# Second buffers and other banks for the mixers' calls, reversed columns in their inverse, and the last adaLN vector summed by VectorE in the gate and up stage

## The chip, the core and the metric

The kernel runs on one core of a Trainium2 chip. The core has five engines that run side by side and wait for one another by semaphores: TensorE (matrix products, results into PSUM), VectorE (DVE in the rows), ScalarE (ACT), GpSimd (POOL) and SyncE (SP), whose queue issues most transfers. The metric is the device time of one execution in microseconds (us).

## What is computed

One block of a backbone with depth 1 on 256 latent tokens and 256 context tokens, width 2048. Six modulation vectors come from the conditioning vector; the sixth, `m_x[5]`, is the gate of the last residual. `_mix` projects to four groups of heads: GLA, Gated DeltaNet (GDN), a short convolution and RWKV-7. The scans run in both directions, first over the context, then over the latent tokens from the context's states.

```python
def _modulation(cond, w, bias):
    m = jax.nn.silu(cond) @ w + bias
    return [a[:, None, :] for a in jnp.split(m, 6, axis=-1)]
...
        o_c, ctx_states = _mix(_modnorm(h_c, norm1_g[l], m_c[0], m_c[1]), h_c.shape[1], zero, lp)
        o_x, _ = _mix(_modnorm(h_x, norm1_g[l], m_x[0], m_x[1]), GRID_W, ctx_states, lp)
        h_x = h_x + m_x[2] * o_x
        h_x = h_x + m_x[5] * _swiglu(_modnorm(h_x, norm2_g[l], m_x[3], m_x[4]), ffn_w_gu[l], ffn_w_down[l])
...
    return _rmsnorm(h_x, final_g)
```

## The kernel before

**Stages.** A first stage (to about 205 us) makes the first two modulation vectors, the norm of the context and eleven early projection tiles. The mixers (to about 1130) hold 16 RWKV directions (4 pairs of heads, 2 directions, context and latent), 8 GDN calls and 4 GLA calls, with the other projections between them. Then come the output projection, gate and up (about 1280 to 1765), down, and the last norm.

**Weights.** A weight tile arrives as float32 (`wraw`), ScalarE rounds it to a high part (`wh`), VectorE subtracts (`wl`), and TensorE makes three products: high by high, high by low, low by high. A projection (`proj`) makes 48 such products of 256 columns from four tiles, in a bank of the pair "big". In gate and up the tiles are 1024 wide (`wide`: four raw buffers, two of each part), while the small set of the mixers (`narrow`: six raw buffers, three of each part) is used in the first turn alone.

**The feed.** Vectors 3, 4, 2 and 5 are fed in this order into the projections: `ada_pieces` gives 64 pieces and a finish for each; `proj` takes two pieces for each of its four weight tiles. A piece is a load of 256 KB into a `wraw` buffer and four products (float32, so two passes) with 32 rows of output, in the bank "ob". The finish of 2 and 5 writes the row to memory, from where it is spread over the partitions (`gate_bc`).

**The inverse.** RWKV and GDN invert four triangular 128x128 matrices a call (`inverse`): VectorE takes the 16x16 blocks of the diagonal (a masked product and a reduction), TensorE spreads their rows (`pr`), and 15 steps of a product and an addition on VectorE make the blocks' inverses (`w_`, `Xc`). RWKV has one kind of triangle in a call. GDN has two lower and two upper ones, and steps over the two kinds apart. Levels of 32 (and 64) then double the blocks on TensorE (`pv`, `px`, `pxt`).

**Banks.** `PB` gives PSUM banks by tag: stream "a" (RWKV) has two "ea" and one "la"; stream "b" (GDN, GLA) one "eb" and one "lb"; the projections have two "big"; the feed has "ob". Eight in all.

**What sets the order.** The code is recorded in the order of the list `ORDER` (with offsets in priority), and a scheduler then gives each engine one fixed order, by priority and by when a buffer is free. A tile with one buffer is given out again when its last reader is done. An engine works strictly in its order, so an instruction that waits holds all behind it.

## Time and profile before

| | us |
|---|---|
| median of three timed runs | 2026.64 |
| lowest and highest | 2023.53, 2029.68 |
| the profiled execution | 2028.87 |
| its span | 2027.1 |
| TensorE busy in the span | 1915.4 |
| VectorE busy | 1343.7 |
| ScalarE busy | 994.5 |

The span is that of the core's instructions. An engine is busy while one of its instructions runs; overlapping instructions count once. TensorE's instructions overlap and their ends are modelled, so a busy TensorE is not one at its peak. The chain that ended last is followed back from the last instruction, at each step to what released it.

### The profile page before, as it was taken

How to read it: one execution, taken by the hardware profiler on the slowest of the kernel's cores; microseconds unless marked ns; L12 is line 12 of the kernel's file. 1: busy time of each engine (PE TensorE's matmuls, PEld its weight loads, DVE VectorE, ACT ScalarE, POOL GpSimd, SP SyncE). 2: the span in 40 equal slices, each digit the busy share in tenths (PEclk: the TensorE clock that was granted, in tenths of full speed). 3: DMA queues.
4: the chain of work that ended last, by engine and by line, in shares of the span. 5: the costliest groups of instructions: out<-in, count | busy, mean ns of one | idle time of the engine just before them, and what ended most of it. 6: DMA issues, size and time to landing. Idle time of an engine off the chain costs nothing.

```text
span 2027.1 us, 37228 instructions
## 1 busy us (share of the span) xinstructions
PE 1915.4 (94%) x13799; PEld 1633.6 (81%) x13800; DVE 1343.7 (66%) x3488; ACT 994.5 (49%) x2029; POOL 161.5 (8%) x199
## 2 busy tenths in 40 slices
PE   5988999799999999999999999899999999999998
PEld 3776877588877878989989978788888888888886
DVE  3446758788788758989897766655555555545554
ACT  2225535555455345465644555555555555544444
POOL 0001001001001000110110000210101010100000
...
GB/s 340 402 292 218 181 224 253 118 138 140 168 204 188 156 193 205 115 110 108 82 118 120 168 184 210 116 187 186 187 187 187 187 187 186 186 231 197 191 194 156
DMA packets 162391, 375.07 MB, mean 185 GB/s; under 512 B 17937, under 2 KB 44049, under 8 KB 157089
## 3 DMA queue, kind: packets, MB, share of 16 engines
...
q8 instruction: 108, 1.77, 0.4%
...
HBM read 360.68 MB, written 11.94 MB: 184 GB/s over the span
## 4 chain that ended last, share of the span: by engine, by line
PE 69%; DVE 10%; DMA 5%; ACT 3%; issue 2%; POOL 0%; SPq 0%; ACTq 0%; DVEq 0%
PE acc L209 36%; PE big L209 12%; PE la L209 7%; PE lb L209 4%; PE ea L209 4%; DVE wl L197 3%; DMA wraw<-in_w_in 3%; PE eb L209 2%; PE ob L209 2%; ACT wh L192 2%; DMA wraw<-in_ada_later 2%; DVE ivaXc L197 1%; DVE ivaw L197 1%; DVE ivbw L197 0%; DVE ivbXc L197 0%
## 5 line engine op out<-in xcount | busy, mean ns | idle before, releaser
L197 DVE TENSOR_TENSOR wl<-wraw,wh 128x512 fp32r<-128x512 f32 x856 | 569.9, 692 | 425.4 <-ACT wh L192 420.7
L192 ACT ACTIVATE wh<-wraw 128x512 fp32r<-128x512 f32 x856 | 510.1, 625 | 543.6 <-PE acc L209 187.3
L209 PE MATMUL acc<-n,wh 128*128 128x512 f32 x1408 | 493.6, 399 | 2.5 <-ACT wh L192 2.5
L209 PE MATMUL acc<-n,wl 128*128 128x256 f32 x1408 | 383.3, 282 | 0.3 <-DVE wl L197 0.3
L209 PE MATMUL big<-nh,wh 128*128 128x256 f32 x1056 | 320.4, 304 | 1.7 <-ACT xs L192 1.3
L209 PE MATMUL big<-nh,wl 128*128 128x256 f32 x1056 | 309.6, 294 | 1.4 <-DVE wl L197 1.4
L209 PEld LDWEIGHTS acc<-n,wh 128*128 128x128 f32 x1408 | 260.0, 189 | 59.6 <-ACT wh L192 2.8
L209 PE MATMUL big<-nl,wh 128*128 128x256 f32 x1056 | 307.7, 292 | 0.0
L209 PEld LDWEIGHTS acc<-n,wl 128*128 128x128 f32 x1408 | 267.2, 190 | 9.7 <-DVE wl L197 1.3
L209 PEld LDWEIGHTS big<-nh,wh 128*128 128x128 f32 x1056 | 200.4, 190 | 27.2 <-issue 19.4
L209 PEld LDWEIGHTS big<-nh,wl 128*128 128x128 f32 x1056 | 200.3, 190 | 8.0 <-issue 2.9
L209 PEld LDWEIGHTS big<-nl,wh 128*128 128x128 f32 x1056 | 200.2, 190 | 5.2 <-issue 4.1
L209 PE MATMUL acc<-wl,hH 128*128 128x512 f32 x352 | 137.1, 389 | 0.0
L209 PE MATMUL acc<-wh,hH 128*128 128x512 f32 x352 | 137.0, 389 | 0.0
L209 PE MATMUL acc<-wh,hL 128*128 128x512 f32 x352 | 137.0, 389 | 0.0
L209 PE MATMUL ob<-wraw,sc 128*32 128x128 f32 x2048 | 106.4, 281 | 16.0 <-DMA wraw<-in_ada_later 12.4
L209 PEld LDWEIGHTS ob<-wraw,sc 128*32 128x32 f32 x2048 | 51.1, 108 | 52.2 <-DMA wraw<-in_ada_later 18.4
L197 POOL TENSOR_TENSOR hL<-sg,hH 128x256 fp32r<-128x256 f32 x44 | 44.6, 1013 | 454.2 <-ACT hH L192 454.2
L209 PEld LDWEIGHTS acc<-wl,hH 128*128 128x128 f32 x352 | 66.1, 188 | 14.2 <-DVE wl L197 0.4
L209 PEld LDWEIGHTS acc<-wh,hL 128*128 128x128 f32 x352 | 66.1, 188 | 13.8
L209 PEld LDWEIGHTS acc<-wh,hH 128*128 128x128 f32 x352 | 66.1, 188 | 13.7
L197 DVE TENSOR_TENSOR wl<-wr,wh 128x1408 fp32r<-128x1408 f32 x16 | 26.0, 1624 | 42.4 <-ACT wh L192 42.4
(468 smaller groups left out, 3123.9 us busy)
## 6 DMA issues: line engine op xcount, KB each, us to landing
wraw<-in_w_gu SPq DMA_DIRECT2D x174, 512.0 KB, 3.1
...
wraw<-in_ada_later SPq DMA_DIRECT2D x256, 256.0 KB, 3.9
...
```

What stands on the lines that cost most here:

```text
L192: A.activation(o, i, AF.Copy)
L197: (e or V).tensor_tensor(out=o, in0=a, in1=b, op=op)
L209: return TE.matmul(o, l, r, start=start, stop=stop)
```

## The change

- The sixth vector (5 in the feed's numbers) is no longer fed to TensorE in the mixers. In gate and up, 64 pieces of 128x512 of its weights are loaded from the third turn on, two recorded in each turn, into the narrow raw buffers; VectorE multiplies each by the conditioning value of its rows and adds it to one of four accumulators, which take two of the three narrow buffers of each part. After the stage TensorE sums the accumulators over the partitions with four products with `ones`, and VectorE adds the bias.
- The inverse gets its diagonal blocks by four ScalarE copies of 32 partitions (`dq`) and two VectorE operations on 64 columns. The upper triangles are held with their columns reversed, so both kinds go through the same 15 steps, on all four matrices at once; the columns are turned back when the blocks are spread.
- `pr` moves from the bank "l" to "e" of its stream; `pxt` of the inverse and `pe` of GDN move from "e" to "big".
- `rw_kt`, `rw_na`, `gd_tok`, `gd_dl` and the ring `bdLM` get a second buffer. The space comes from `ident`, which is left out of the second copy of the constants, and from one tag for two outputs.

The diff, cut to its core (the other hunks repeat second buffers, or shift offsets of constants by 128):

```diff
@@ -154,9 +156,12 @@
     first = a[:, :, 0:2].transpose(3, 1, 0, 2, 4).reshape(KT * P, KT * 2 * P)
-    later = w[:, 2 * D:].reshape(KT, P, 4, 4, 4, P).transpose(2, 4, 0, 1, 3, 5).reshape(4 * 4 * KT * P, 512)
+    later = w[:, 2 * D:5 * D].reshape(KT, P, 3, 4, 4, P).transpose(2, 4, 0, 1, 3, 5).reshape(3 * 4 * KT * P, 512)
+    last = w[:, 5 * D:].reshape(KT * P, 4, 512).transpose(1, 0, 2).reshape(4 * KT * P, 512)
+    later = np.concatenate([later, last])
     return np.ascontiguousarray(first), np.ascontiguousarray(later)
...
@@ -296,13 +301,13 @@
             row = wraw()
-            if ci in (2, 5):
+            if ci == 2:
                 G.memset(row, 0.0)
                 for g in range(4):
                     nc.sync.dma_start(row[32 * g:32 * g + 1, :], ada_b[0:1, ci * D + g * 512: ci * D + (g + 1) * 512])
                 tt(row, ps, row, ADD)
                 for g in range(4):
-                    nc.sync.dma_start(gate_dram[ci // 4:ci // 4 + 1, g * 512:(g + 1) * 512], row[32 * g:32 * g + 1, :])
+                    nc.sync.dma_start(gate_dram[0:1, g * 512:(g + 1) * 512], row[32 * g:32 * g + 1, :])
                 return
...
@@ -652,11 +659,13 @@
             for u, low in enumerate(lowers):
                 groups.setdefault(low, []).append(u)
 
-            t5 = mk(mx, [P, 4, 8, 16], iv + "L", 1)
-            tt(t5, nL.rearrange("p u (b c) -> p u b c", c=16),
-               blk16.unsqueeze(1).unsqueeze(3).to_broadcast([P, 4, 8, 16]), MUL)
+            dq = mk(mx, [P, 4, 32], iv + "Q", 1)
+            for q in range(4):
+                sl = slice(32 * q, 32 * q + 32)
+                acopy(dq[sl], nL[sl, :, sl])
             dg = mk(mx, [P, 4, 16], iv + "D", 1)
-            V.tensor_reduce(out=dg, in_=t5.rearrange("p u b c -> p u c b"), axis=mybir.AxisListType.X, op=ADD)
+            ts(dg, dq[:, :, 0:16], even, MUL)
+            stt(dg, dq[:, :, 16:32], odd, dg, MUL, ADD)
 
             dx = mk(mx, [P, 4, 15], iv + "d", 1)
             for low, us in groups.items():
...
@@ -667,32 +676,27 @@
             sel = mk(mx, [P, 4, 8, 15], iv + "R", 1)
             tt(sel, bcast(dx, 2, 8), row8.unsqueeze(1).unsqueeze(3).to_broadcast([P, 4, 8, 15]), MUL)
 
-            pr = PB([P, 480], "l")
+            pr = PB([P, 480])
             mm(pr, ones16, sel.rearrange("p u i j -> p (u i j)"))
             bc_ = mk(mx, [P, 4, 8, 15], iv + "C", 1)
             acopy(bc_.rearrange("p u i j -> p (u i j)"), pr)
             Xc = mk(mx, [P, 4, 16], iv + "Xc", 1)
-            G.tensor_copy(Xc, bcast(id16, 1, 4))
+            for low, us in groups.items():
+                G.tensor_copy(Xc[:, us[0]:us[-1] + 1], bcast(id16 if low else id16r, 1, len(us)))
             w_ = mk(mx, [P, 4, 16], iv + "w", 1)
             for st in range(15):
-                step = []
-                for low, us in groups.items():
-
-                    n, u = 15 - st, slice(us[0], us[-1] + 1)
-                    if low:
-                        i = 15 - st
-                        js, e = slice(0, n), bc_[:, u, st, 0:n] if i >= 8 else bc_[:, u, i, 14:14 - n:-1]
-                    else:
-                        i = st
-                        js, e = ((slice(15, i, -1), bc_[:, u, i, 0:n]) if i < 8 else
-                                 (slice(i + 1, 16), bc_[:, u, 15 - i, i:15]))
-                    tt(w_[:, u, js], e, Xc[:, u, i:i + 1].to_broadcast([P, len(us), n]), MUL)
-                    step.append((u, js))
-                for u, js in step:
-                    tt(Xc[:, u, js], Xc[:, u, js], w_[:, u, js], ADD)
+                n = i = 15 - st
+                e = bc_[:, :, st, 0:n] if i >= 8 else bc_[:, :, i, 14:14 - n:-1]
+                tt(w_[:, :, 0:n], e, Xc[:, :, i:i + 1].to_broadcast([P, 4, n]), MUL)
+                tt(Xc[:, :, 0:n], Xc[:, :, 0:n], w_[:, :, 0:n], ADD)
             X = mk(mx, [P, 4, P], iv + "X", 2)
-            tt(X.rearrange("p u (b c) -> p u b c", c=16), bcast(Xc, 2, 8),
-               blk16.unsqueeze(1).unsqueeze(3).to_broadcast([P, 4, 8, 16]), MUL)
+            for low, us in groups.items():
+                us_ = slice(us[0], us[-1] + 1)
+                tt(X[:, us_].rearrange("p u (b c) -> p u b c", c=16),
+                   bcast(Xc[:, us_] if low else Xc[:, us_, ::-1], 2, 8),
+                   blk16.unsqueeze(1).unsqueeze(3).to_broadcast([P, len(us), 8, 16]), MUL)
             nxt = iv + "XT", 1 if len(levels) == 2 and rhs is not None else 2
             XT = mk(mx, [P, 4, P], *nxt)
             pt = PB([P, 4, P], "l")
...
@@ -729,7 +733,7 @@
                 if not last and (rhs is None or b != levels[-2]):
-                    pxt = PB([P, 4, P])
+                    pxt = PB([P, 4, P], "big")
                     for c in range(4):
...
@@ -943,12 +947,12 @@
                     TE.transpose(pk[:, c], f2(KK[:, c]), ident)
-                kt_ = mk(mx, [P, 4, P], "rw_kt", 1)
+                kt_ = mk(mx, [P, 4, P], "rw_kt", 2)
                 acopy(kt_, pk)
 
                 w = P if s == 1 else 64
                 def turned(t, tag):
-                    pt, o = PB([P, 4, P]), mk(mx, [P, 4, P], tag, 1)
+                    pt, o = PB([P, 4, P]), mk(mx, [P, 4, P], tag, 2 if tag == "rw_na" else 1)
                     for c in range(4):
...
@@ -1064,7 +1068,7 @@
                 l2(q, P ** -0.5)
-            tok = mk(mx, [P, 4, P], "gd_tok", 1)
+            tok = mk(mx, [P, 4, P], "gd_tok", 2)
             pt = PB([P, 4, P])
...
@@ -1084,7 +1088,7 @@
                 mm(pbc[:, d], ident[:, 32 + r:33 + r].to_broadcast([P, P]), sm["smd"][d])
-            dl = mk(mx, [P, 4, P], "gd_dl", 1)
+            dl = mk(mx, [P, 4, P], "gd_dl", 2)
             R = mk(mx, [P, 4, 2, P], "gd_R", 1)
...
@@ -1125,7 +1129,7 @@
                     ts(Fg[:, u].rearrange("p a b -> p (a b)")[:, :w], src, sm["nbe"][:, d, h, c:c + 1], MUL)
-                pe = PB([P, 2, 2, P])
+                pe = PB([P, 2, 2, P], "big")
                 for c in range(2):
...
@@ -1338,10 +1342,10 @@
         rings = rws.enter_context(tc.tile_pool(name="rings", bufs=1, reuse_waits="tile"))
-        bdLM = Ring(rings, "bdLM", [P, 4, 2, 2, 64], 1)
+        bdLM = Ring(rings, "bdLM", [P, 4, 2, 2, 64], 2)
         bdKh = Ring(rings, "bdKh", [P, 4, 2, 64], 1)
         bdE = Ring(rings, "bdE", [P, 4, 2, 64], 1)
-        for ci in (3, 4, 2, 5):
+        for ci in (3, 4, 2):
             feed += ada_pieces(ci, lambda shape: mk(pb, shape, "ob", 1), mx)
...
@@ -1460,7 +1464,25 @@
     p3 = ctx.enter_context(tc.tile_pool(name="p3", bufs=1, reuse_waits="tile"))
     hH = mk(p3, [P, FT, T], "hH", 1, F32R)
     hL = mk(p3, [P, FT, T], "hL", 1, F32R)
+    gacc = [mk(narrow[0], [P, 512], t, narrow[2]) for t in ("wh", "wh", "wl", "wl")]
+    def gate_piece(i):
+        kt, q = divmod(i, 4)
+        raw = mk(narrow[0], [P, 512], "wraw", narrow[3])
+        r0 = ((3 * 4 + q) * KT + kt) * P
+        nc.sync.dma_start(raw, ada_later[r0:r0 + P, :])
+        if kt == 0:
+            ts(gacc[q], raw, sc[:, 0, 0:1], MUL)
+        else:
+            stt(gacc[q], raw, sc[:, kt, 0:1], gacc[q], MUL, ADD)
+    gate_todo = list(range(4 * KT))
     for f in range(FT):
+        if f > 1:
+            for i in gate_todo[:2]:
+                gate_piece(i)
+            del gate_todo[:2]
 
         pg = [mk(ps2, [P, 2, T], "acc", 8) for _ in range(2)]
         for k0, nk, bufs in ((0, 8, wide), (8, 4, narrow), (12, 4, narrow)) if f == 0 else ((0, 8, wide), (8, 8, wide)):
...
@@ -1493,7 +1515,12 @@
     with tc.issue_after(silu.ins):
         A.preload_act_table_set("natural_log_exp_and_others")
     g5 = mk(p5, [P, D], "g5")
-    gate_bc(1, g5)
+    nc.sync.dma_start(g5, ada_b[0, 5 * D:6 * D].partition_broadcast(P))
+    for q in range(4):
+        ps = mk(ps2, [P, 512], "acc", 8)
+        mm(ps, ones, gacc[q])
+        sl = slice(q * 512, (q + 1) * 512)
+        tt(g5[:, sl], ps, g5[:, sl], ADD)
     fg = mk(p5, [P, D], "fg")
     nc.sync.dma_start(fg, final_g.partition_broadcast(P))
     ss = [mk(p5, [P, 4], f"ss{j}", 1) for j in range(2)]
```

TensorE, during one GDN inverse over the context (`lb` products with `ivb` tiles) beside an RWKV inverse (`la`, `iva`). Before:

```order
L209 MATMUL lb_5675<-ivbX_5657,ivbW_5673 128x128 x4
L209 MATMUL eb_5681<-ivbW_5673,ivbX_5657 128x128 x4
L209 MATMUL la_5461<-rw_na_5372,ivaX_5457 128x64 x4
L209 MATMUL big_6911<-nl_831_4125,wh_6974 128x256
L209 MATMUL big_6911<-nh_830_4124,wl_6975 128x256
L209 MATMUL lb_5691<-ivbXT_5686,ivbL_5689 128x128 x4
L209 MATMUL la_5468<-ivaW_5466,ivaL_5459 128x64 x4
L209 MATMUL big_6911<-nh_834_4134,wh_6974 128x256
L209 MATMUL big_6911<-nl_835_4135,wh_6974 128x256
L209 MATMUL big_6911<-nh_834_4134,wl_6975 128x256
```

Now, in the same call:

```order
L214 MATMUL lb_5605<-ivbX_5586,ivbW_5603 128x128 x4
L214 MATMUL big_5611<-ivbW_5603,ivbX_5586 128x128 x4
L214 MATMUL la_5929<-ivaXT_5920,ivaL_5927 128x128 x4
L214 MATMUL lb_5621<-ivbXT_5616,ivbL_5619 128x128 x4
L214 MATMUL la_5936<-ivaX_5918,ivaW_5934 128x128 x2
L1228 MATMUL eb_5737<-ident_64,gd_k_5725 128x128 x2
L214 MATMUL la_5936<-ivaX_5918,ivaW_5934 128x128 x2
L214 MATMUL lb_5628<-ivbX_5610,ivbW_5626 128x128 x3
L214 MATMUL eb_5742<-gd_kq_5721,gd_dl_5740 128x256
L214 MATMUL lb_5628<-ivbX_5610,ivbW_5626 128x128
L214 MATMUL big_5634<-ivbW_5626,ivbX_5610 128x128
```

Between the two streams' products stood projection products (`big<-nl,wh` and the like); now the products of a GLA call (`eb`) stand there, `pxt` is in "big", and no projection product.

VectorE, at the start of the first GDN inverse (`ivb`) beside an RWKV inverse. Before, with the reduction and the first step on two matrices twice (`128x2x15 x2`):

```order
L659 TENSOR_REDUCE ivbD_2781<-ivbL_2779 128x64
L197 TENSOR_TENSOR wl_2440<-wraw_2437,wh_2439 128x512
L201 TENSOR_SCALAR ivbd_2783<-ivbD_2781,consts_89 128x30 x2
L206 SCALAR_TENSOR_TENSOR ivbd_2783<-ivbD_2781,consts_89,ivbd_2783 128x30 x2
L197 TENSOR_TENSOR ivbL_2866<-gd_dl_2764,consts_89 128x512
L197 TENSOR_TENSOR wl_2475<-wraw_2472,wh_2474 128x512
L197 TENSOR_TENSOR ivbR_2788<-ivbd_2783,consts_89 128x480
L197 TENSOR_TENSOR ivaR_1633<-ivad_1630,consts_89 128x480
L197 TENSOR_TENSOR ivaL_1681<-bdLM_254_1533,consts_89 128x512
L197 TENSOR_TENSOR wl_2505<-wraw_2502,wh_2504 128x512
L197 TENSOR_TENSOR ivbw_2796<-ivbC_2792,ivbXc_2794 128x2x15 x2
L203 TENSOR_SCALAR rw_z_1754<-ea_1755,par_63 128x256
```

Now, from the second of the two operations that replace the reduction:

```order
L211 SCALAR_TENSOR_TENSOR ivbD_2794<-ivbQ_2789,consts_89,ivbD_2794 128x64
L206 TENSOR_SCALAR ivaD_1633<-ivaQ_1628,consts_89 128x64
L206 TENSOR_SCALAR ivbd_2797<-ivbD_2794,consts_89 128x30 x2
L211 SCALAR_TENSOR_TENSOR ivbd_2797<-ivbD_2794,consts_89,ivbd_2797 128x30 x2
L211 SCALAR_TENSOR_TENSOR ivaD_1633<-ivaQ_1628,consts_89,ivaD_1633 128x64
L202 TENSOR_TENSOR ivbR_2802<-ivbd_2797,consts_89 128x480
L206 TENSOR_SCALAR ivad_1636<-ivaD_1633,consts_89 128x60
L211 SCALAR_TENSOR_TENSOR ivad_1636<-ivaD_1633,consts_89,ivad_1636 128x60
L202 TENSOR_TENSOR wl_2450<-wraw_2447,wh_2449 128x512
L202 TENSOR_TENSOR ivaR_1639<-ivad_1636,consts_89 128x480
L202 TENSOR_TENSOR ivbw_2811<-ivbC_2806,ivbXc_2808 128x4x15
L202 TENSOR_TENSOR ivbXc_2808<-ivbXc_2808,ivbw_2811 128x4x15
```

The reduction is gone, `ivaD` and `ivbD` are made from `ivaQ` and `ivbQ`, and a step is one product and one addition on four matrices (`128x4x15`).

VectorE in gate and up, about one turn of the loop (`wl` are the low parts, two halves each). Before:

```order
L197 TENSOR_TENSOR wl_16259<-wraw_16256,wh_16258 128x512 x2
L197 TENSOR_TENSOR wl_16267<-wraw_16264,wh_16266 128x512 x2
L197 TENSOR_TENSOR wl_16320<-wraw_16317,wh_16319 128x512 x2
L197 TENSOR_TENSOR ga_16304<-acc_16206,ga_16304 128x256
L197 TENSOR_TENSOR wl_16328<-wraw_16325,wh_16327 128x512 x2
L197 TENSOR_TENSOR up_16305<-acc_16207,up_16305 128x256
L197 TENSOR_TENSOR sg_16306<-ga_16304,up_16305 128x256
L197 TENSOR_TENSOR wl_16368<-wraw_16365,wh_16367 128x512 x2
```

Now, where the sixth vector is summed (`wh_15567` and the like are its accumulators):

```order
L202 TENSOR_TENSOR wl_16268<-wraw_16265,wh_16267 128x512 x2
L202 TENSOR_TENSOR ga_16246<-acc_16148,ga_16246 128x256
L211 SCALAR_TENSOR_TENSOR wh_15567<-wraw_17867,sc_82,wh_15567 128x512
L202 TENSOR_TENSOR wl_16276<-wraw_16273,wh_16275 128x512 x2
L202 TENSOR_TENSOR up_16247<-acc_16149,up_16247 128x256
L211 SCALAR_TENSOR_TENSOR wh_15568<-wraw_17870,sc_82,wh_15568 128x512
L202 TENSOR_TENSOR sg_16248<-ga_16246,up_16247 128x256
L211 SCALAR_TENSOR_TENSOR wl_15569<-wraw_17982,sc_82,wl_15569 128x512
L202 TENSOR_TENSOR wl_16316<-wraw_16313,wh_16315 128x512 x2
L211 SCALAR_TENSOR_TENSOR wl_15570<-wraw_17985,sc_82,wl_15570 128x512
L202 TENSOR_TENSOR wl_16324<-wraw_16321,wh_16323 128x512 x2
L211 SCALAR_TENSOR_TENSOR wh_15567<-wraw_18097,sc_82,wh_15567 128x512
```

One or two sums stand ahead of each pair of splits; the 64 are spread over about the first fourteen turns.

## Rows read from the trace of the kernel before

**Rows 1.** page, its first line.

```profile
span 2027.1 us, 37228 instructions
```

**Rows 2.** stretch, length, busy us (instructions) of PE, PEld, DVE, ACT, POOL; clock, DMA.

```profile
205.00:640.00 435.00, 402.65 (x3715) 335.64 (x3714) 332.02 (x1136) 223.01 (x495) 29.27 (x46) 0.96 0.57 176
640.00:800.00 160.00, 153.99 (x1449) 128.18 (x1447) 119.50 (x368) 70.45 (x144) 13.31 (x16) 1.00 0.63 196
800.00:1130.00 330.00, 317.07 (x2418) 294.97 (x2418) 284.91 (x886) 176.95 (x374) 36.96 (x44) 1.00 0.35 110
```

**Rows 3.** page, part 4: the chain that ended last, by engine.

```profile
PE 69%; DVE 10%; DMA 5%; ACT 3%; issue 2%; POOL 0%; SPq 0%; ACTq 0%; DVEq 0%
```

**Rows 4.** tile ob: busy in 640 to 800; the finishing additions, first and last.

```profile
640.00:800.00 160.00, 27.09 (x512) 12.60 (x512) 1.37 (x2) 0.00 (x0) 1.00 0.63 196
L197 DVE TENSOR_TENSOR wraw<-ob,wraw x2: 682/686/691, 640.4 to 795.8; 128x512 f32<-128x512 f32 x2
```

**Rows 5.** the chain by line in 640 to 800, then in 800 to 1000.

```profile
by line: DMA wraw<-in_w_in 15.4%; PE big L209 13.1%; PE la L209 12.8%; PE lb L209 6.6%; PE ob L209 5.5%; DVE wl L197 5.3%; ACT wh L192 4.6%; PE ea L209 4.2%; DMA wraw<-in_ada_later 3.9%; issue 3.8%; DVE ivaXc L197 3.4%; DVE ivaw L197 2.6%; 
by line: PE big L209 25.1%; PE la L209 18.1%; PE lb L209 9.6%; PE ea L209 8.0%; DVE wl L197 7.1%; PE eb L209 6.0%; issue 3.1%; ACT wh L192 1.5%; DMA gd_rk<-xr_d_k 1.5%; DVE ivaw L197 1.3%; DVE ivaXc L197 1.2%; DVE ivaX L197 1.1%; DVE ivbD L
```

**Rows 6.** waits in 640 to 800, ScalarE's, then SyncE's queue: us, times, longest.

```profile
ACT wh L192 <- DMA wraw<-in_w_in: 22.8, 16, 3.3
SPq L292 <- PE ob L209: 25.5, 25, 2.4
```

**Rows 7.** VectorE in 205 to 1130: shape, count, busy us, mean ns, idle before.

```profile
L197 DVE TENSOR_TENSOR wl<-wraw,wh 128x512 fp32r<-128x512 f32 x231 | 160.9, 698 | 59.7 <-ACT wh L192 55.7 <-PE ob L209 1.6 <-PE eb L209 0.8
L197 DVE TENSOR_TENSOR ivaL<-bdLM,consts 128x512 f32<-128x512 f32 x47 | 33.1, 704 | 0.0
L659 DVE TENSOR_REDUCE ivaD<-ivaL 128x64 f32<-128x512 f32 x15 | 15.4, 1024 | 0.1
L201 DVE TENSOR_SCALAR ivad<-ivaD,consts 128x60 f32<-128x60 f32 x16 | 3.9, 246 | 0.1
L206 DVE SCALAR_TENSOR_TENSOR ivad<-ivaD,consts,ivad 128x60 f32<-128x60 f32 x16 | 4.4, 274 | 0.0
L197 DVE TENSOR_TENSOR ivbw<-ivbC,ivbXc 128x30 f32<-128x30 f32 x16 | 2.3, 182 | 0.7 <-ACT ivbC L192 0.7
L197 DVE TENSOR_TENSOR ivbXc<-ivbXc,ivbw 128x2 f32<-128x2 f32 x16 | 2.0, 155 | 0.0
L197 DVE TENSOR_TENSOR ivaw<-ivaC,ivaXc 128x60 f32<-128x60 f32 x16 | 3.7, 228 | 4.6 <-ACT ivaC L192 4.4
L197 DVE TENSOR_TENSOR ivaXc<-ivaXc,ivaw 128x4 f32<-128x4 f32 x16 | 3.1, 192 | 0.1
```

**Rows 8.** ScalarE in 205 to 1130: a small copy, and a wait.

```profile
L192 ACT ACTIVATE gd_S<-lb 128x128 f32<-128x128 f32 x24 | 6.6, 274 | 15.9 <-PE lb L209 15.8
ACT rw_kt L192 <- PE la L209: 5.2, 6, 1.9
```

**Rows 9.** three other stretches, columns as in rows 2; the last is GB/s.

```profile
700.00:750.00 50.00, 49.06 (x449) 40.32 (x448) 23.42 (x56) 19.00 (x38) 1.61 (x3) 1.00 0.45 143
800.00:950.00 150.00, 144.13 (x1092) 132.98 (x1092) 137.12 (x461) 82.65 (x174) 19.73 (x23) 1.00 0.35 108
1400.00:1450.00 50.00, 50.00 (x285) 43.48 (x284) 27.75 (x49) 25.59 (x53) 4.08 (x4) 1.00 0.56 186
```

**Rows 10.** the chain in 815 to 835: start us, us, what.

```profile
821.88 11.26 PE big L209 x94
```

**Rows 11.** VectorE's 128x512 operation; ones products; a gap in gate and up.

```profile
L206 DVE SCALAR_TENSOR_TENSOR gd_qe<-gd_qe,par,gd_tok 128x512 f32<-128x512 f32 x2 | 1.5, 746 | 0.0
L209 PE MATMUL lb<-gd_tok,ones 128*128 128x512 f32 x4 | 2.2, 627 | 0.0
1402.65 1.29 DVE L197 TENSOR_TENSOR wl<-wraw,wh 128x512 fp32r<-128x512 f32 x2 [1.61 <-ACT wh L192]
```

**Rows 12.** page, part 2: GB/s in 40 slices.

```profile
GB/s 340 402 292 218 181 224 253 118 138 140 168 204 188 156 193 205 115 110 108 82 118 120 168 184 210 116 187 186 187 187 187 187 187 186 186 231 197 191 194 156
```

More of the change, by code (lines that the diff above doesn't have):

```diff
@@ L87, in _const_array @@
     add("half", np.concatenate([q < 8, q >= 8], 1))
+    add("side", np.concatenate([i // 16 % 2 == 0, i // 16 % 2 == 1], 1))
+    add("id16r", np.arange(P)[:, None] % 16 == 15 - np.arange(16)[None, :])
     r = np.arange(32)[None, :]
@@ L275, in rsqrt @@
         act(o, o, AF.Exp, scale=-0.5)
-    gate_dram = mk(dram, [2, D], "gated")
+    gate_dram = mk(dram, [1, D], "gated")
     def ada_pieces(ci, bank_of, tmp):
@@ L337, in block_kernel @@
     kp = mix.enter_context(tc.tile_pool(name="kp", bufs=1, reuse_waits="tile"))
-    C = mk(kp, [P, NCONST], "consts")
+    C = mk(kp, [P, NCONST - P], "consts")
     sw = mk(kp, [P, 3072], "sw")
     def cc(name, n=P):
-        return C[:, COFF[name]:COFF[name] + n]
+        return C[:, COFF[name] - P:COFF[name] - P + n]
     lev = {b: cc(f"lev{b}") for b in LEVS}
@@ L351, in block_kernel @@
     lo8, hi8 = cc("half", 2)[:, 0:1], cc("half", 2)[:, 1:2]
+    even, odd = cc("side", 2)[:, 0:1], cc("side", 2)[:, 1:2]
+    id16r = cc("id16r", 16)
     class Ring:
@@ L468, in block_kernel @@
         for i, dst in ((0, C), (1, sw)):
-            nc.sync.dma_start(dst, (consts, small)[i])
+            nc.sync.dma_start(dst, (consts[:, P:], small)[i])
         for f in done:
@@ L1181, in gla @@
             if s == 1:
-                v = mk(mx, [P, 4, 2, 64], "gd_tok", 1)
+                v = mk(mx, [P, 4, 2, 64], "gd_tok", 2)
                 for hh in range(2):
@@ L1197, in gla @@
             else:
-                v = mk(mx, [P, 2, 2, P], "gd_tok", 1)
+                v = mk(mx, [P, 2, 2, P], "gd_tok", 2)
                 for hh in range(2):
@@ L1224, in gla @@
                         TE.transpose(pt[:, c], ke[:, c * P:(c + 1) * P], ident)
[L1225 removed]
+                    kt_ = mk(mx, [P, 4, P], "gd_dl", 2)
                     acopy(kt_[:, :2], pt)
@@ L1257, in gla @@
                     TE.transpose(pt[:, c], KE[:, c].rearrange("p a b -> p (a b)"), ident)
-                kt_ = mk(mx, [P, 4, P], "gd_dl", 1)
+                kt_ = mk(mx, [P, 4, P], "gd_dl", 2)
                 acopy(kt_, pt)
@@ L1279, in gla @@
             f4 = lambda t: t.rearrange("p c h j -> p (c h j)")
-            sq = mk(mx, [P, 512], "gd_tok", 1)
+            sq = mk(mx, [P, 512], "gd_tok", 2)
             act(sq, f4(y), AF.Square)
@@ L1299, in short_conv @@
             conv(o, pr, [pc("scconv", tap * 4 + t) for tap in range(3)], 1)
-            yo = t1("sc_y", 2)
+            yo = t1("y_o", 2)
             tt(yo, pcol(nHL, "c_b", t), o, MUL)
```

3 lines of the change are left out of this document (1 added, 2 removed).

## The prediction

> **What bounds the kernel now.** I read the profile in this order: busy time by stage, the chain that ended last, then waits and durations inside the stage that the change touches most. The profiled execution took 2028.87 us, of which the span is 2027.1 [rows 1]; the median of the three timed runs is 2026.64, 2.2 us less. The sum below is made against 2028.87 and moved by -2.2 at the end. The mixers, from about 205 to 1130 us, are 925 us of the span. There TensorE is busy 873.7 us and VectorE 736.4 [rows 2]: two engines near their limit, which take turns. The chain of the whole span gives TensorE 69%, VectorE 10%, DMA 5%, ScalarE 3% [rows 3]. Gate-and-up and down are different: in 1400 to 1450 TensorE is busy 50.00 of 50 us and VectorE 27.75 [rows 9].
>
> **The change, part by part.**
>
> *1. The last adaLN vector leaves the mixers.* Its 64 pieces are the last of the feed, between the finish of the vector before (640.4 us) and its own (795.8) [rows 4]. In 640 to 800 they are 512 TensorE instructions (64 pieces, four products, two passes), 27.1 us busy [rows 4], where TensorE is busy 153.99 of 160 us [rows 2]. Their loads leave SyncE's queue too. In 640 to 800 that queue waits 25.5 us on the ob products, which hold the shared wraw buffers, and ScalarE waits 22.8 us for projection weights [rows 6]. The chain there has 15.4% in the projections' loads, 5.5% in ob and 3.9% in the pieces' loads; in 800 to 1000, after the last piece, none of the three is among the lines listed, which go down to 1.1% [rows 5]. Bounds: 15 us (5.5 + 3.9% of 160) and 40 us (with the 15.4%). I take **-26 us**, the products' own time, since TensorE is busy 96% there and could hardly give more. The finish (one 0.69 us addition, eight tiny DMAs) hides.
>
> *2. The inverse, VectorE.* 24 calls (16 RWKV, 8 GDN) lose a masking product (0.70 us, an ivaL row) and a reduction (1.02), and gain a tensor_scalar and a scalar_tensor_tensor on 128x64, for which the 128x60 rows stand: 0.25 and 0.27 [rows 7]. That is 1.2 us x 24 = 29 us. The eight GDN calls had 60 small steps on two matrices, 182 ns at the widest and 155 at the narrowest; now 30 steps on four, for which the RWKV rows stand: 228 and 192 [rows 7]. By durations 60 x 0.168 - 30 x 0.21 = 3.8 us a call, 30 in all; by busy time (2.3 and 2.0 us for 16, against 3.7 and 3.1) 60 x 0.135 - 30 x 0.21 = 1.8 a call, 14 in all. I take 20, so VectorE loses 49 of 736 us. How much is on the path? VectorE's 10% of the span is 203 us, nearly all in the mixers: 22% of 925. 0.22 x 49 = **-11 us**; bounds 0 (TensorE holds the end throughout) and -49.
>
> The widths show that half the elements do not cost half the time: 30 against 60 columns is 182 against 228 ns [rows 7]. [...]
>
> *3. The diagonal, ScalarE.* Four copies of 32 partitions x 128 a call, 96 in all. The nearest row is a 128x128 copy at 274 ns [rows 8]: 26 us on an engine busy 470 of 925 [rows 2]. Queued behind them are the weight splits (wh), and TensorE waits for those. ScalarE has 3% of the chain, 61 us, 6.6% of the mixers: **+2 us**, between 0 and 26. As a step, four copies and two small operations (1.6 us) replace 1.72 us; the latency of a call is unchanged.
>
> *4. Second buffers, other banks.* What waited on a buffer can be seen in one place: the copy to rw_kt waits 5.2 us, six times, for products that read the old one [rows 8]. Most other waits are for data. The inverse's pxt and the GDN product pe go to "big", pr to "e"; so "eb" is free and the next call's front can run during an inverse, as the order of TensorE shows. **-4 us**; bounds 0 and -51 (all of TensorE's idle time in the mixers, 925 - 873.7). The cost of the same edits is in 5.
>
> *5. The order.* "big" is the projections' own pair of banks, and the faster mixers run ahead of the projections. Counted in TensorE's order, runs of 96 or more projection products with nothing but adaLN products between hold 237 products before and 1338 now, and the longest run grows from 123 to 461. In such a run TensorE is full and VectorE is not: 94 products took 11.26 us [rows 10], so a projection of 48 takes 5.75 us, while its four splits (0.70 each [rows 7]) give VectorE 2.8. In 700 to 750 VectorE is busy 23.4 of 50; in 800 to 950, where the two are mixed, 137.1 of 150 [rows 9]. As a balance: the long runs take 1338 x 0.120 = 160 us and contain 28 projections' splits, 78 us; VectorE's other 736 - 49 - 78 = 609 us need 609/u outside them, u being VectorE's busy share there. With u = 0.91 (as in 800 to 950) the mixers last 829 us, with 0.80 (their mean now, 736/925) 921, with 0.77 951. I expect second buffers to bring u to about 0.83: 894, that is -31, near the sum of 1 to 4 (-39) and a loss of **+10 us** from the runs, which I take; bounds 0 and +68 (23 more projections, 2.95 us of idle VectorE each).
>
> *6. Gate and up.* 60 scalar_tensor_tensors and 4 tensor_scalars on 128x512: 0.75 us each [rows 11], 48 us on VectorE, four or five in a turn of the loop (64 products; 285 take 50 us [rows 9], so 11.2 us), so VectorE goes from 6.2 to 9.7 us of 11.2. They stand in the gaps before a pair of splits, like the 1.61 us in which VectorE now waits for ScalarE [rows 11]; such a gap holds two. SyncE issues each piece's load between two weight loads; the piece waits for one of six small buffers, and the next weight load waits behind it. DMA moves 186 GB/s there [rows 9] and has to move about 295 for some 14 turns (4.7 pieces of 0.26 MB more in 11.2 us); the kernel moves 340 to 400 in its first slices [rows 12]. **0 us**; if the cover is gone, up to 48. The end adds four fp32 products with "ones" where TensorE is never idle: two such products are 2.2 us [rows 11], four are **+4 us**; the additions hide beside the first down products.
>
> *Sum:* -26 - 11 + 2 - 4 + 10 + 0 + 4 = -25. 2028.9 - 25 = 2003.9, on the median's scale **2002 us**.
>
> **The rivals.**
>
> *A. The runs of projections eat the gain (slower).* VectorE-bound stretches and TensorE-bound runs follow each other instead of overlapping. For it: 1338 against 237 products in long runs, and VectorE half idle in 700 to 750. Against it: VectorE has 49 us less to do, and more calls overlap outside the runs. It decides at u = 0.80, below which the mixers (with the +4) are no shorter. At u = 0.77 they last 951 us: 2026.6 + 26 + 4 = 2057. [...]
>
> *B. The order fits better than I think (much faster).* u = 0.88 to 0.91: mixers of 852 to 829 us, 2026.6 - 73 + 4 = 1958 to -96 + 4 = 1935. For it: two more calls in flight. Against it: TensorE alone has 873.7 - 27 = 847 busy us in the mixers, overlapped ends included, so I stop at 1965.
>
> *C. Gate and up stalls.* A piece that lands late holds VectorE, the splits behind it and TensorE. At 0.3 us for each of 64 pieces it is +19: 2021. For it: 9.7 of 11.2 us. Against it: the gaps hold the work, and six buffers let loads run ahead.
>
> *D. Nothing moves.* The freed time goes into other waits and the +4 stays: 2026 to 2031.
>
> **How the numbers follow.** About 0.3% (6 us) is what a measurement of this kernel can tell from no change. The forecast, 1985 to 2018: 0.47. B, below 1985: 0.12. C: 0.05, half of it still over 0.3% faster. D: 0.08. A, above 2033: 0.28. So faster 0.62, same 0.10, slower 0.28. The range leaves 0.1 at each end: below 1972 most of B is out, above 2052 the worse half of A.
>
> **What would show it.** Step 1: no ob products after the finish of the third vector of the feed, and ScalarE's waits for in_w_in loads gone from the middle of the mixers. Step 2: VectorE busy in the mixers about 690 us. Step 5: in long runs VectorE near 23 of 50, outside above 0.80. Step 6: TensorE still 50 of 50 in the turns with pieces. The prediction is wrong if u falls below 0.80, if TensorE idles in gate and up, or if ScalarE's copies hold the splits.

## The result, and the profile after

The changed kernel takes 2178.03 us (median of four runs, 2176.28 to 2182.75), the kernel before 2027.06 on the same chip: a ratio of 1.075, with a 95% interval of 1.0725 to 1.0774. The forecast was 2002 us, its range ended at 2052, and slower had a chance of 0.28. The profiled execution took 2176.92 us.

The page of the changed kernel, to be held against [rows 1], [rows 3] and [rows 12]: span, granted clock of TensorE (PEclk, 9 is full), DMA and GB/s in 40 slices of 54 us, and the chain by engine.

```profile
span 2175.1 us, 36148 instructions
PE 1967.4 (90%) x13295; PEld 1659.6 (76%) x13296; DVE 1372.9 (63%) x3323; ACT 1032.2 (47%) x2125; POOL 157.8 (7%) x207
...
PEclk7999999879985999898799989999999999999999
DMA  8967563520770353130007537679655555566554
GB/s 351 396 238 244 164 221 103 177 80 6 228 256 22 107 173 125 60 96 21 9 2 237 171 106 224 192 251 324 240 186 188 188 184 187 188 216 194 194 194 155
...
PE 75%; DVE 11%; DMA 5%; ACT 5%; issue 2%; POOL 1%; SPq 0%; ACTq 0%; DVEq 0%; POOLq 0%
```

From the tenth to the twenty-first slice the traffic falls to 6, 22, 21, 9 and 2 GB/s in places, and the clock falls in the same part (5 tenths in the thirteenth slice). First, where the time lies. The stretch from 205 us to the first product of gate and up, and the stretch from there to the last product (columns: stretch, length, busy us and instructions of PE, PEld, DVE, ACT, POOL; clock, DMA share, GB/s). Before:

```profile
205.00:1274.00 1069.00, 1011.20 (x8345) 876.03 (x8344) 834.54 (x2572) 552.15 (x1174) 85.69 (x112) 0.98 0.52 160
1274.00:2017.00 743.00, 740.22 (x3871) 632.00 (x3871) 408.55 (x693) 370.07 (x729) 62.12 (x58) 1.00 0.57 186
```

After:

```profile
205.00:1417.00 1212.00, 1057.42 (x7814) 899.26 (x7815) 816.31 (x2332) 586.31 (x1259) 78.36 (x118) 0.91 0.40 127
1417.00:2165.00 748.00, 744.64 (x3884) 634.07 (x3882) 455.86 (x762) 370.64 (x730) 65.41 (x58) 1.00 0.61 206
```

Of 148 us, 143 lie ahead of gate and up. There VectorE has 18 us less to do, TensorE 531 instructions less, and yet TensorE is busy 46 us longer and idle 97 us longer (1212 - 1057.4 against 1069 - 1011.2). The longer busy time goes with a lower clock, 0.91 against 0.98 (step 5 below).

Second, what is missing there: the same 154 us of both kernels, with the columns as above. Before:

```profile
979.00:1133.00 154.00, 147.75 (x1130) 138.14 (x1129) 127.21 (x374) 78.70 (x167) 15.72 (x18) 1.00 0.38 120
```

Of that, the instructions on `nh` tiles alone, which are two of three products of every projection (columns: PE, PEld, DVE, ACT):

```profile
979.00:1133.00 154.00, 86.59 (x426) 67.51 (x427) 0.00 (x0) 0.00 (x0) 1.00 0.38 120
```

After, with the stretch that follows:

```profile
979.00:1133.00 154.00, 106.55 (x610) 87.97 (x610) 107.88 (x367) 58.29 (x131) 15.55 (x23) 0.82 0.03 10
1133.00:1280.00 147.00, 143.79 (x1156) 138.74 (x1156) 92.87 (x183) 77.61 (x160) 9.20 (x9) 1.00 0.56 178
```

And after, the instructions on `nh` tiles in the first of the two:

```profile
979.00:1133.00 154.00, 0.00 (x0) 0.00 (x0) 0.00 (x0) 0.00 (x0) 0.82 0.03 10
```

In 154 us the changed kernel makes **no projection product at all**; then, in 1133 to 1280, some 950 of them. Between projections there are six such stretches of 47 to 155 us, 506 us in all. Before there is one of 72 us and one of 13; the one of 72 us (the norm of the latent tokens, where no projection can be ready) is in both. The other five of the changed kernel, all engines (the second is the norm's):

```profile
302.00:355.00 53.00, 42.67 (x321) 29.37 (x320) 43.27 (x162) 30.79 (x71) 5.73 (x10) 0.87 0.38 120
383.00:450.00 67.00, 50.51 (x339) 33.57 (x338) 52.27 (x159) 42.96 (x104) 5.12 (x7) 0.78 0.49 150
458.00:539.00 81.00, 72.82 (x540) 61.86 (x540) 67.05 (x250) 39.97 (x94) 7.10 (x15) 0.92 0.12 39
630.00:733.00 103.00, 71.02 (x411) 50.83 (x404) 66.64 (x221) 40.24 (x89) 9.03 (x15) 0.67 0.19 62
883.00:930.00 47.00, 33.47 (x181) 27.28 (x179) 29.66 (x99) 14.63 (x28) 3.12 (x7) 0.78 0.10 32
```

In the six, VectorE, which was to be the limit there, is busy 367 of 505 us: 0.73.

Third, what stands at the ends of such a stretch. The instructions on tiles of the tag `big` in the changed kernel, around the start and the end of this one (columns: minimum, median and maximum duration in ns, then first and last start):

```profile
L214 PE MATMUL big<-ivbW,ivbX x8: 275/275/275, 1013.8 to 1015.0; 128*128 128x128 f32 x8
...
L214 PE MATMUL big<-nl,wh x5: 279/282/285, 975.7 to 978.3; 128*128 128x256 f32 x5
...
L214 PE MATMUL big<-gd_Fg,gd_tok x6: 379/380/435, 1128.0 to 1135.1; 128*128 128x256 f32 x6
...
L214 PE MATMUL big<-nl,wh x5: 280/282/283, 1133.7 to 1139.7; 128*128 128x256 f32 x5
```

The last projection before it ends at 979 us. 35 us later come the first products of `pxt` (`big<-ivbW,ivbX`) of two GDN calls, and the projections begin again with the last `pe` (`big<-gd_Fg,gd_tok`) of the second call. The other four (the sixth is the norm's) have this shape too. The tiles themselves hold a bank for 2 to 4 us (a `pxt` from its first product at 1013.7 to the end of its copy at 1016.0, a `pe` from 1126.2 to its last reader's end at 1130.5); the stretch lasts 155.

### The profile page after: what moved, and what is told of

It reads as the page before. It is cut to its first block, busy times and chain, and to the rows that moved or that the text cites. A ratio compares the mean times of both kernels' runs of the same rounds, so it can differ in the third digit from the quotient of the medians.

```text
span 2175.1 us, 36148 instructions
## 1 busy us (share of the span) xinstructions
PE 1967.4 (90%) x13295; PEld 1659.6 (76%) x13296; DVE 1372.9 (63%) x3323; ACT 1032.2 (47%) x2125; POOL 157.8 (7%) x207
## 4 chain that ended last, share of the span: by engine, by line
PE 75%; DVE 11%; DMA 5%; ACT 5%; issue 2%; POOL 1%; SPq 0%; ACTq 0%; DVEq 0%; POOLq 0%
PE acc L214 36%; PE big L214 16%; PE la L214 7%; PE ea L214 5%; PE lb L214 3%; PE ob L214 2%; DVE wl L202 2%; PE eb L214 2%; ACT wh L197 2%; DMA wraw<-in_w_in 1%; DMA wraw<-in_ada_later 1%; DMA ad<-in_ada_first 1%; DVE ivaXc L202 1%; DVE ivaw L202 1%; PE pt L214 0%
## 5 line engine op out<-in xcount | busy, mean ns | idle before, releaser
L214 PE MATMUL big<-nh,wh 128*128 128x256 f32 x1056 | 313.9, 298 | 7.6 <-DVE y_o L202 4.4
L214 PE MATMUL ob<-wraw,sc 128*32 128x128 f32 x1536 | 89.8, 300 | 28.6 <-DMA wraw<-in_ada_later 24.8
L214 PEld LDWEIGHTS ob<-wraw,sc 128*32 128x32 f32 x1536 | 38.6, 112 | 65.3 <-DMA wraw<-in_ada_later 35.2
L202 DVE TENSOR_TENSOR ivaw<-ivaC,ivaXc 128x60 f32<-128x60 f32 (+14 forms) x240 | 47.7, 199 | 9.9 <-ACT ivaC L197 6.8
```

The costliest lines, as they stand in the source:

```text
L202: (e or V).tensor_tensor(out=o, in0=a, in1=b, op=op)
L214: return TE.matmul(o, l, r, start=start, stop=stop)
```

## The experiments

Times are medians; the difference is to the kernel before in the same comparison (2027.8 to 2029.9 us).

| run | what is changed against before | us | difference | ratio, 95% interval |
|---|---|---|---|---|
| e1 | `pxt`, `pe` in `big` | 2226.19 | +196.8 | 1.0943 to 1.0983 |
| e2 | all but that | 2037.84 | +8.5 | 1.0028 to 1.0058 |
| e3 | inverse | 2039.78 | +10.4 | 1.003 to 1.0059 |
| e4 | vector | 2006.80 | -22.6 | 0.987 to 0.9911 |
| e5 | `pxt`, `pe` in a bank of their own | 2074.75 | +44.9 | 1.0189 to 1.0242 |
| e6 | `pe` in `big` | 2223.73 | +193.9 | 1.0924 to 1.0981 |
| e7 | e4 + shared tag `y_o` | 2032.75 | +2.9 | 0.9993 to 1.0037 |
| e8 | e2 without shared tag and GDN's buffers | 2012.91 | -16.9 | 0.9885 to 0.994 |
| e9 | e4 + 30 steps | 2001.22 | -28.3 | 0.9847 to 0.9894 |
| e10 | e4 + new diagonal | 2001.08 | -28.4 | 0.9846 to 0.9892 |
| e11 | e4 + RWKV buffers | 2000.35 | -29.2 | 0.9848 to 0.9886 |
| e12 | the changed kernel, states by GpSimd | 2173.93 | +144.4 | 1.0679 to 1.0763 |
| e13 | e4 + inverse | 2012.38 | -15.4 | 0.9898 to 0.9939 |
| e14 | e8 with `pr` in `l` | 1995.91 | -31.9 | 0.9818 to 0.9853 |
| e15 | e13 with `pr` in `e` | 2006.26 | -21.5 | 0.9865 to 0.9907 |
| e16 | e4 + 30 steps + RWKV buffers | 1995.45 | -32.3 | 0.9817 to 0.9853 |

### The change in four parts: e1 to e4

e1, the kernel before with two words changed:

```diff
-                    pxt = PB([P, 4, P])
+                    pxt = PB([P, 4, P], "big")
...
-                pe = PB([P, 2, 2, P])
+                pe = PB([P, 2, 2, P], "big")
```

> The kernel before with one edit: the tiles pxt of the inverse and pe of GDN are taken from the pair of banks 'big' (the projections' own) instead of 'e'. No second buffers, the old inverse, the sixth vector still in the mixers. Theory K (banks): this edit alone makes the loss, because the scheduler now finds a 'big' bank free for a projection only between pxt and pe, sets the projections back and plays them in long runs (1153 projection products in runs of 96 or more, 237 before, 1338 in the changed kernel). It expects 2130 to 2190 us, stretches of the mixers with TensorE busy under 40 of 50 us, almost no DMA traffic and a granted clock below 0.9. Rival S (second buffers): the calls run ahead of the projections because tiles come free earlier; then this edit alone is worth 2010 to 2045 us. Rival V (the shorter feed sets the order): also 2010 to 2045.

Measured: 2226.19 us, above the range, since the other parts take some 46 us back in the changed kernel. The longest stretch of e1 without projections, all engines:

```profile
1041.00:1201.00 160.00, 114.43 (x638) 94.84 (x637) 119.92 (x442) 54.44 (x119) 15.09 (x22) 0.80 0.04 11
```

Its instructions on `nh` tiles:

```profile
1041.00:1201.00 160.00, 0.26 (x2) 0.06 (x1) 0.00 (x0) 0.00 (x0) 0.80 0.04 11
```

The picture of the changed kernel, without second buffers and with the old inverse. This edit alone makes the loss.

e2, the changed kernel with these two lines taken back:

> The changed kernel with pxt and pe back in 'e'; second buffers, the new inverse with its pr in 'e', and the sixth vector in gate and up all stay. Theory K: the long runs are gone (300 products in runs of 96 or more), so the sum of the other steps of the prediction holds: 2027 - 26 - 11 + 2 - 4 + 4 = 1992, between 1970 and 2012 us, TensorE's granted clock at 1.00 through the mixers. Rivals S and V: the loss stays, 2110 us or more.

2037.84 us: the great loss is gone, so rivals S and V fall; but 1992 was expected, and TensorE still has a lower clock in places (0.59 in the stretch below). There is one stretch left that before doesn't have. No instruction of e2 reads an `nh` tile in it; all engines:

```profile
1115.00:1152.00 37.00, 20.02 (x72) 14.88 (x72) 15.70 (x40) 10.81 (x26) 2.24 (x2) 0.59 0.06 18
```

e3, the inverse alone, with `pr` in `l`:

```diff
-            tt(t5, nL.rearrange("p u (b c) -> p u b c", c=16),
+            for q in range(4):
+                sl = slice(32 * q, 32 * q + 32)
+                acopy(dq[sl], nL[sl, :, sl])
...
+                tt(w_[:, :, 0:n], e, Xc[:, :, i:i + 1].to_broadcast([P, 4, n]), MUL)
+                tt(Xc[:, :, 0:n], Xc[:, :, 0:n], w_[:, :, 0:n], ADD)
```

> The kernel before with the new inverse alone (diagonal by four ScalarE copies and two small VectorE operations, one kind of triangle, 30 steps on four matrices); pr stays in 'l', pxt and pe in 'e'. The prediction's steps 2 and 3 give -11 + 2: 2010 to 2026 us, and VectorE about 49 us less busy in the mixers (1295 instead of 1344 in the span). If the copies hold the weight splits behind them on ScalarE (rival to step 3), 2035 us or more. The order is nearly that of before (244 products in long runs).

2039.78 us: the kernel is 10 us slower, as the rival to step 3 would have it; e10 below tests that rival. VectorE has less to do, but by 28 us and not by 49 (step 2 below). Its busy time (DVE) and ScalarE's (ACT) in the span of e3:

```profile
PE 1923.5 (94%) x13800; PEld 1635.4 (80%) x13800; DVE 1315.6 (65%) x3256; ACT 1022.0 (50%) x2125; POOL 157.8 (8%) x207
```

e4, the vector alone (the hunks of `ada_pieces`, of the packing and of gate and up):

> The kernel before with the last adaLN vector alone moved to VectorE in gate and up. The prediction's steps 1 and 6 give -26 + 4: 2005 us, between 1995 and 2020. If the pieces stall gate and up (rival C), TensorE is not 50 of 50 us in the turns with pieces and the time is 2020 or more. If a feed that ends earlier lumps the projections (rival V; 439 products in runs of 96 or more), the time is 2040 or more.

2006.80 us, within 2 us of what was expected. The step was right.

### How two tiles hold up the projections: e5, e6, e12

e5, the same two tiles in a bank of their own:

```diff
-            tag = tag if tag == "big" else tag + cur[0]
-            return mk(pb, shape, tag, 2 if tag in ("big", "ea") else 1)
+            tag = tag if tag in ("big", "gx") else tag + cur[0]
+            return mk(pb, shape, tag, 2 if tag == "ea" else 1)
...
-                    pxt = PB([P, 4, P])
+                    pxt = PB([P, 4, P], "gx")
```

> The kernel before with pxt and pe taken out of 'e', as in e1, but into a bank of their own, 'gx', so that the projections keep one bank, 'big', instead of the pair (8 banks in all, as ever; the output projection takes one of each). Theory R (rotation): tiles of one tag get its buffers in the order in which they are recorded, so in e1 a projection recorded behind a GDN call had to wait for the call's pxt and pe, and TensorE had no projections left to put between the call's own steps. With a bank of their own the tie is gone, though the projections have a bank less: no stretch over 25 us without projections except the one in the norm of the latent tokens (344 to 416 us before), 2020 to 2090 us. Theory O (occupation): what costs is that a bank of the two is taken from the projections; then it is as slow as e1 or slower, 2150 us or more.

2074.75 us. The projections have one bank where e1 gave them a share of two, and the kernel is 151 us faster than e1. But for the norm, the longest stretches are of 16 us, like the second of these (instructions on `nh` tiles); the first is the norm:

```profile
345.00:413.00 68.00, 0.22 (x1) 0.28 (x1) 7.21 (x15) 8.08 (x16) 0.87 0.47 141
758.00:774.00 16.00, 0.35 (x2) 0.31 (x3) 0.00 (x0) 0.00 (x0) 0.79 0.72 225
```

Most of the cost is not the bank taken (e5 takes one too, and is 45 us slower than before), but the common order.

e6, `pe` alone in `big`:

> The kernel before with pe alone in 'big' (16 small tiles, two in each of the eight GDN calls), pxt stays in 'e'. Theory R: a tie at one place of the call is enough, since every projection recorded behind the call waits for it: again a stretch without projections at each GDN call, 300 us or more of such stretches in sum (507 in the changed kernel, 86 before), 2120 to 2230 us. Theory O: half of the tiles, and these are held for a shorter time, so half of the loss of e1 or less: 2050 to 2110 us.

2223.73 us, as slow as e1 with half of its tiles. Instructions on `nh` tiles in its longest stretch:

```profile
1034.00:1195.00 161.00, 0.44 (x2) 0.22 (x2) 0.00 (x0) 0.00 (x0) 0.80 0.04 11
```

One tie in a call is enough. So theory R stands: the tiles of a tag are given its buffers in turn, in the order in which the code records them. A projection recorded behind a GDN call can't have its bank before the call's last `pe`, and TensorE has nothing to put between the steps of this call and of those beside it.

TensorE's order shows the tie itself. The number in a tile's name rises as the code is recorded. Before, TensorE works on the projection `big_6911` just behind `eb_5681`, a `pxt` that was recorded far ahead of it. In the changed kernel it takes up all 122 tiles of `big` in rising order of their numbers: behind the projection `big_4157` come eight tiles `pxt` and `pe` of two GDN calls (4932 to 5680), and only then the next projection, `big_6220`.

e12 is the changed kernel with the loads of the starting states on another queue, because SyncE's queue waits long for them there. In the changed kernel, in 205 to 1290 (columns: us, times, longest):

```profile
SPq L540 <- PE lb L214: 120.7, 4, 96.7
SPq L604 <- DVE wl L202: 117.3, 94, 11.5
SPq L540 <- DVE rw_S L206: 109.9, 6, 47.0
```

```diff
-            nc.sync.dma_start(t, SD[key])
+            G.dma_start(t, SD[key])
```

> The changed kernel with the loads of the starting states (gd_S, rw_S; 20 loads) issued on GpSimd's queue instead of SyncE's. In the trace of the changed kernel SyncE's queue waits 120.7 and 109.9 us at these loads, once 96.7 us in one piece, and projection weights are queued behind. Theory Q (the queue holds the weights, and so the projections): 2030 to 2090 us. Theory R (the projections are held by the order of the banks, and the loads' waits are only its shadow): 2150 to 2190 us, with the same stretches without projections.

2173.93 us, as before the edit (2178). The queue now stands at the weight loads themselves (L604), for splits that hold the raw buffers (in 205 to 1416, where the changed kernel has 137.9 us of this wait, 14.0 at the longest):

```profile
SPq L604 <- DVE wl L202: 274.4, 98, 140.6
```

The long waits of SyncE's queue were a shadow of the missing projections, though they looked like a cause.

### The same tie in SBUF: e7, e8

```diff
-            yo = t1("sc_y", 2)
+            yo = t1("y_o", 2)
```

> e4 (the sixth vector alone moved) with one more edit of the changed kernel, which the prediction passed over: the output of the short convolution takes the tag y_o, shared with the GLA outputs, instead of its own, sc_y. Theory R: the same tie in SBUF: the short convolution, recorded near the GLA calls, has to wait in y_o's order, so its last four projections (192 products) are played after the last GLA call instead of beside it. It expects 2020 to 2035 us (e4: 2007), with a stretch of 25 to 45 us without projections behind 1050 us. If the tag is harmless: 2003 to 2012 us.

2032.75 us: this one word costs 26 us on top of e4. All engines in e7's stretch without projections:

```profile
1114.00:1154.00 40.00, 21.25 (x79) 15.48 (x78) 17.01 (x43) 11.85 (x29) 2.24 (x2) 0.62 0.07 23
```

In e4 the last projections run beside the last GLA call instead (instructions on `nh` tiles):

```profile
1100.00:1133.00 33.00, 29.48 (x162) 24.76 (x161) 0.00 (x0) 0.00 (x0) 1.00 0.57 180
```

e8 is e2 without the shared tag; `gd_tok` and `gd_dl` have one buffer again, for the space.

> e2 (all of the change but the banks) without the shared tag; for its space the second buffers of gd_tok and gd_dl are given up, those of rw_kt, rw_na and bdLM stay. Theory R: the 38 us without projections that e2 has at 1115 us are gone, 2000 to 2022 us. If e2's loss against e4 (31 us) comes from the new inverse or from the RWKV buffers instead, 2028 us or more.

2012.91 us: the stretch at 1115 us is gone, and 25 us with it, though two second buffers went too.

VectorE's order shows this tie too. In e7 it writes all tiles of `y_o` in rising order of their numbers; in e4 it writes `sc_y_14155` and `sc_y_14385` ahead of `y_o_13805`.

### The inverse and the buffers: e9 to e11, e13 to e16

e9 takes the 30 steps without the new diagonal, e10 the new diagonal without the steps, e11 the second buffers of `rw_kt`, `rw_na` and `bdLM`, each on top of e4.

> e4 (the sixth vector alone moved) with half of the new inverse: upper triangles held with reversed columns, 30 steps on four matrices in a GDN call; the diagonal stays a masked product and a reduction on VectorE. In e3's trace the GDN steps took 46.1 us as a sum of durations and before 80.7, but before they overlap each other, so VectorE gains less. Theory A (VectorE's saved time is worth little, ScalarE's added copies cost): 1996 to 2008 us, no slower than e4 (2007). Theory B (the steps cost, since two chains that overlapped are now one chain): 2012 us or more.

> e4 with the other half of the new inverse: the diagonal blocks by four ScalarE copies and two small VectorE operations, the steps as before. VectorE has some 28 us less to do, ScalarE 29 us more (96 copies of 306 ns in e3's trace). Theory A: the copies stand ahead of weight splits and of the spills' copies on ScalarE, and cost more than the +2 us of the prediction: 2012 to 2025 us. Theory B: 1998 to 2008 us.

> e4 with the second buffers of rw_kt, rw_na and bdLM, and the constants cut by 128 columns to make room; the old inverse, all banks as before, tag sc_y kept. The prediction's step 4 put all second buffers at -4 us (bounds 0 and -51), for waits of 5.2 us on rw_kt. It expects 1999 to 2007 us. If the calls run further ahead of the projections with them (the prediction's rival A without the banks), 2012 us or more.

2001.22, 2001.08 and 2000.35 us: 6 us each against e4. The intervals of the three overlap with that of e4, so each gain by itself is at the edge of what these runs can tell. In e10 theory A falls: ScalarE's copies, of which this row of e10 has most (columns as in [rows 8]), do no harm there.

```profile
L196 ACT ACTIVATE ivaQ<-bdLM 32x128 f32<-32x128 f32 x60 | 18.3, 305 | 3.7 <-DVE bdLM L201 3.1
```

The steps of the GDN calls on VectorE (instructions on `ivbw` tiles, in 205 to 1130: stretch, length, busy us and instructions of VectorE; clock, DMA). Before, then in e3:

```profile
205.00:1130.00 925.00, 58.87 (x480) 0.98 0.51 156
```

```profile
205.00:1130.00 925.00, 46.03 (x240) 0.98 0.50 155
```

> e4 with the whole new inverse, pr still in 'l'. If the gains of the two halves add (2007 - 6 - 6): 1991 to 1999 us. If ScalarE's copies cost once VectorE's steps are short (e3's loss): 2008 us or more.

> e8 with pr back in 'l' (the vector, the whole inverse, the RWKV buffers). If pr's bank is the cause (in 'e' it stands in the rotation of the call's other tiles): 1985 to 2000 us. If it isn't: 2005 to 2020 us, as e8 (2013).

> e13 with pr in 'e'. If pr's bank is the cause of e8's loss: 10 to 20 us more than e13. If not: within 5 us of e13.

> e4 with the 30 steps (e9) and the RWKV buffers (e11), the old diagonal, pr in 'l', pxt and pe in 'e', tag sc_y kept. If the gains add: 1990 to 1998 us. If two such edits hinder each other by the order that the scheduler finds: 2003 us or more.

e13, 2012.38 us: the two halves together are 5.6 us slower than e4, where each alone was 6 faster; its interval lies apart from those of e9 and e10, and e3 agrees. e15 against e13: `pr` in `e` gains 6, at the edge of the noise; e8 against e14: it costs 15. So `pr`'s bank has no fixed price. With the RWKV buffers the inverse costs nothing (e14, 1995.91, against e11), and the steps and the RWKV buffers add to within 3 us (e16, 1995.45). These edits are worth some 6 us each, and their combinations miss the sums by as much or more, either way; that the order which the scheduler finds does this is argued, not shown. Why e13 is slower than e9 and e10 is open: its second theory, that ScalarE's copies cost once the steps are short, has the number. With the buffers the copies cost nothing (e14 has them, e16 doesn't); without them no run parts that theory from a worse order. e14 and e16 beat both kernels; e14 is the change without its two banks, the shared tag, GDN's buffers and `pr`'s bank.

## Why the prediction was wrong, point by point

**Step 1, the vector: right.** -26 + 4 with step 6 was -22; e4 measured -22.6. The sum is nearer than its terms, which is luck: in e4's trace the stretch from 205 us to gate and up is 31 us shorter than before, and what follows 7 us longer.

```profile
205.00:1243.00 1038.00, 976.79 (x7830) 860.04 (x7829) 827.15 (x2570) 548.70 (x1171) 83.50 (x111) 0.98 0.48 149
```

**Step 6, gate and up: right.** The stretch from its first product to the end grew from 743 to 748 us, and the prediction had +4. Turns with pieces in the changed kernel, against [rows 9]:

```profile
1450.00:1500.00 50.00, 50.00 (x285) 43.51 (x285) 47.16 (x76) 25.48 (x53) 7.01 (x5) 1.00 0.94 323
1500.00:1550.00 50.00, 50.00 (x285) 43.25 (x284) 43.85 (x72) 26.60 (x55) 5.24 (x4) 1.00 0.88 306
```

TensorE stays at 50.00 with VectorE at 47 and 323 GB/s (estimated: 295). Rival C did not come.

**Step 2, the inverse on VectorE: too large.** 49 us of work were forecast; e3's VectorE is busy 1315.6 us in the span, before 1343.7: 28. The diagonal's own instructions (on `ivaL`, `ivbL`, `ivaD` and `ivbD`) fell by 29 us, as forecast. The term of the steps was 20 and measured 58.87 - 46.03 = 12.8 in e3. Together that is 42 us; the total fell by 14 less. Part of what was saved had run beside other instructions of VectorE: before, in 205 to 1130, it ran nothing else in 28.6 of the steps' 58.87 us; that this is most of the 14 was not shown. In the kernel before, 480 instructions of 167 ns at the median make some 80 us of durations in 58.87 us of busy time: the two kinds of triangle overlapped each other already. The prediction reckoned the steps both ways, 30 us by durations and 14 by busy time, and took 20 between them. As a sum of durations they fell by 34.7 us (80.7 to 46.0 in e3), but busy time fell by 12.8, so durations may not be summed where independent instructions overlap. On the path, the halves gave 5.6 and 5.7 us, in sum near the -11 + 2 of steps 2 and 3; joined they gave a loss (e3, e13), so that forecast didn't hold for the edit as it was made.

**Step 3, ScalarE's copies: right in work.** 26 us of work were forecast, and e3's ScalarE is busy 1022.0 against 994.5 us. The +2 on the path was not measured by itself: e10 holds the saved reduction too.

**Step 4, buffers and banks: the step that failed.** It set second buffers and banks at -4 in one line, and left what the same edits cost to step 5, at +10. e11 shows -6.6 for the RWKV buffers. But the banks are not of that kind: e1 prices them at **+197**. The prediction said that `eb` is free and that the next call's front can run during an inverse. TensorE's order bears that out, and it is beside the point, because the prediction did not ask who else takes buffers of the tag that the tiles move *to*, and in what order.

**Step 5, the order: the right sign, far too small, the wrong cause.** The 1338 products in long runs were seen, and a sign of being wrong that the prediction named, u below 0.80, is what came. But the runs were priced by VectorE's idle time in them (+10, at most +68), and rival A at 2057 us, 30 us above the kernel before; measured are 151. Three things were off. First, the cause: what the prediction put down to faster mixers that run ahead was an effect of the banks almost alone (1153 products in e1, with the old inverse and single buffers; 300 in e2, with the new ones). Second, u: the balance took 0.83 and its rival 0.77, since more calls in flight were to keep VectorE busy outside the runs. The six stretches have 0.73, and the balance itself, solved for the 143 us that were lost, gives 609 / (925 + 143 - 160) = 0.67. The calls are chains; with no projection between their steps both engines wait for each other. Third, a term was missing: the granted clock was lower where TensorE idled. In 630 to 733 of the changed kernel it is 0.67, in 690 to 704 of that stretch 0.50, and the calls' own products take longer just where they hold the end. A group of them there, and the same group in 965 to 1118 with its median:

```profile
L214 PE MATMUL la<-ivaXT,ivaL 128*128 128x128 f32 x16 | 4.0, 428 | 0.7 <-ACT ivaXT L197 0.7
```

```profile
L214 PE MATMUL la<-ivaXT,ivaL x32: 275/275/583, 965.1 to 1118.4; 128*128 128x128 f32 x32
```

The 16 of the first stretch took 428 ns in the mean (the eight in 692 to 694, where the clock was 0.50, 421 at the median and 582 at the slowest); of the 32 in the second, half took 275 and the slowest 583. Over the mixers and the output projection TensorE is busy 46 us longer and, with the 27 us of products that left, some 73 us like for like. In that part it is busy 162 us at a granted clock of 0.50, before 26. By the group's 421 against 275 ns, 47 of the 73 us are the clock, and up to 68 if every product took twice as long there, as the slowest of the eight did (both are estimates); the rest is open. e1, with the same products as before, agrees: 1092.40 us busy against 1011.20, at a clock of 0.90.

```profile
205.00:1472.00 1267.00, 1092.40 (x8354) 920.51 (x8347) 851.96 (x2574) 561.49 (x1174) 78.41 (x112) 0.90 0.43 135
```

Idle time (97 us) and low clock are two prices of one cause.

Rival A had stretches of the two kinds follow each other instead of overlapping, and the traces show what that does: mixed (before, 979 to 1133), 154 us hold 147.75 us of TensorE and 127.21 of VectorE; parted (the changed kernel, the same stretch), 106.55 and 107.88.

**Passed over: the shared tag.** The description of the change names "one tag for two outputs" as a source of space, and the prediction gave it no cost. It is the same tie in SBUF, and e7 measures 26 us.
